# RWKV chunk chain with both heads in one matmul, and the first two input tiles in token halves

## The chip, the cores and the metric

One core of a Trainium2 chip runs one decoder block in fp32. The metric is device time in microseconds of one execution, lower is better. The kernel before takes 2918.94 us (median of 3 runs, 2916.89 to 2919.65).

## The reference, cut to what matters

The block normalises `x` (512 tokens, width 2048), projects it with `w_in`, runs RWKV-7 time mixing and sliding-window attention on parts of the projection, merges them with gates, and ends with a gated convolutional feed-forward. Of this the change touches the projection's beginning and the RWKV recurrence:

```python
h = rms_norm(x, norm1_g[l])
z = h @ w_in[l]
...
def step(state, inp):
    r_t, k_t, v_t, w_t, ka_t, kb_t = inp
    sa = jnp.einsum('bhvk,bhk->bhv', state, ka_t)
    state = (state * w_t[:, :, None, :] + sa[..., None] * kb_t[:, :, None, :]
             + v_t[..., None] * k_t[:, :, None, :])
    y = jnp.einsum('bhvk,bhk->bhv', state, r_t)
    return state, y
```

There are 16 heads of 64 channels. The kernel computes the recurrence in 8 chunks of 64 tokens (`NCH`, `C`), two heads (a pair, 128 partitions) at a time.

## The kernel before, in words

**Projection.** `w_in` is read in column tiles of 128 (`z_tiles`): first the attention keys and values (`c_ka`, `c_va`, two of each), then the queries, the low-rank inputs, and for each pair of heads k, r, v; the 32 gate tiles come last and serve as filler. Every product in fp32 is made of three fp32r matmuls, high times high, low times high, high times low (L259 to L261), 128 by 512 each, 16 input slices `k` to a tile, so 48 matmuls. `load_w` (L237) fetches four slices of weights through a ring of 4 raw buffers and splits them: ACT makes the high part (L244), DVE the low part (L245). After every third call it also issues one step of the running sums that later stages need (`sums_along`, L228 and L229).

**Start.** `x` comes in four row blocks of 128 tokens. Each half of the tokens (two blocks) is squared on ACT (L294), scaled on DVE (L297), turned over by 32 PE transposes (L304) into PSUM tiles `ps_x` of a ring of 6, and split by ACT (`xhi`, L306) and DVE (`xlo`, L307). The first tile's matmuls run over all 512 tokens, so they stand behind both halves.

**RWKV pair.** `early` (L556) makes a pair's inputs, `late` (L616) its chunks. `late` first builds block matrices and inverts a triangular system with fp16 matmuls (L690, L691); then comes the chain over the 8 chunks. For each chunk: `psG` from the state `SV` and `AB`, one matmul for each head into its own 64 partitions (L744); a copy to `G` on DVE (L746); `psU` with the inverse, one matmul for both heads (L748); copies to `UV`, the first head's on ACT (L749), the second's on DVE (L750); `psS`, again a matmul for each head (L755); and the new state on DVE (L757). The chunk's outputs are two more matmuls for each head (L765 with `MM`, L767 with `BAR`), all into one PSUM tile from the ring `bulk` of 3; after the last chunk it is split into `yhl` (L769) for `final`. The unused blocks of `SV` and `UV` hold what the state and the values need beside the own block, so that the contraction over 128 rows gives two terms at once.

**Order.** The framework's scheduler interleaves the engines' streams at build time: the chain's matmuls stand between those of gate and projection tiles. Each engine then runs its own stream strictly in order and waits at semaphores; what stands behind a waiting instruction waits too. Instructions given to `pin` keep their program order.

Of the kernel before, what the change touches and what calls it, by code (L numbers as in the profile page):

```python
# [20 lines left out]
NT = S // P  # L21
HD = 64
C = 64
NCH = S // C
BLK = 128
WIN = 128
RMS_EPS = 1e-6
# [108 lines left out]
def block_kernel(ctx: ExitStack, tc: tile.TileContext, d: Dims, a: dict, out: bass.AP):  # L136
    nc = tc.nc
    act, dve, pool, pe, sync = nc.scalar, nc.vector, nc.gpsimd, nc.tensor, nc.sync
    NK, NP, NQ, NKV, NF = d.NK, d.NP, d.NQ, d.NKV, d.NF
# [16 lines left out]
    ident = const.tile([P, P], F32, name="ident")  # L156
# [5 lines left out]
    cst = cstp.tile([P, NCONST - P], F32, name="cst")  # L162
# [6 lines left out]
    p0 = xin.enter_context(tc.tile_pool(name="x0", bufs=1))  # L169
    xt = [p0.tile([P, d.D], F32, name=f"xi{t}") for t in range(NT)]  # L170
# [35 lines left out]
    def split(hi, lo, src, pin=free):  # L206
        pin(act.activation(hi, src, AF.Copy))
        pin(dve.tensor_tensor(lo, src, hi.bitcast(F32) if hi.dtype == F32R else hi, op=ALU.subtract))
# [28 lines left out]
    def load_w(src):  # L237
# [4 lines left out]
        hi = wp["hl"].tile([P, 512], F32R, name="whi", tag="whi")[:, :n].rearrange("p (k c) -> p k c", c=ncol)  # L242
        lo = wp["hl"].tile([P, 512], F32R, name="wlo", tag="wlo")[:, :n].rearrange("p (k c) -> p k c", c=ncol)
        act.activation(hi, raw, AF.Copy)  # L244
        dve.tensor_tensor(lo, raw, hi.bitcast(F32), op=ALU.subtract)  # L245
        wp["n"] += 1
        if wp["n"] % wp["step"] == 0:
            sums_along()()
        return hi, lo

    def project(acc, src, xhi, xlo, pre=()):
        nk = src.shape[1]
        for k0 in range(0, nk, 4):
            n = min(4, nk - k0)
            whi, wlo = pre[k0 // 4] if k0 // 4 < len(pre) else load_w(src[:, k0 : k0 + n])
            for j in range(n):
                k = k0 + j
                first, last = k == 0, k == nk - 1
                pe.matmul(acc, whi[:, j], xhi[:, k], start=first, stop=False)  # L259
                pe.matmul(acc, whi[:, j], xlo[:, k], start=False, stop=False)  # L260
                pe.matmul(acc, wlo[:, j], xhi[:, k], start=False, stop=last)  # L261


    act.dma_start(par, a["par"])
    sync.dma_start(sinkb, a["attn_sinks"].rearrange("(o h) -> o h", o=1).to_broadcast([P, d.HQ]))
    sync.dma_start(cst, a["cst"][:, P:])
# [17 lines left out]
    if True:  # L284
        xhi = by_k(big(big1, "xhi", "h1"))
        xlo = by_k(big(big1, "xlo", "l1"))
        zt = {c: a["w_z"][i].rearrange("p (k c) -> p k c", c=P) for i, c in enumerate(d.z_tiles())}
        with tc.tile_pool(name="x0_ps", bufs=6, space=PSUM) as ps0:
            ssum = p0.tile([P, NT], F32, name="ssum")
            HT = NT // 2  # L290
            for h in range(2):
                for t in range(h * HT, (h + 1) * HT):
                    sq = p0.tile([P, d.D], F32, name="sqx", tag="sqx", bufs=1)
                    act.activation(sq, xt[t], AF.Square, accum_out=ssum[:, t : t + 1])  # L294
                r = rsqrt_small(p0, ssum[:, h * HT : (h + 1) * HT], 1.0 / d.D, RMS_EPS)
                for t in range(HT):
                    dve.tensor_scalar(xt[h * HT + t], xt[h * HT + t], r[:, t : t + 1], None, op0=ALU.mult)  # L297
            first = {d.c_ka: [load_w(zt[d.c_ka][:, k0 : k0 + 4]) for k0 in range(0, min(NK, 12), 4)]}
            for h in range(2):
                hs = slice(h * HT * P, (h + 1) * HT * P)  # L300
                for k in range(NK):
                    ps = ps0.tile([P, HT * P], F32, name="ps_x", tag="x")
                    for t in range(HT):
                        pe.transpose(ps[:, t * P : (t + 1) * P], xt[h * HT + t][:, k * P : (k + 1) * P], ident)  # L304
                    g = col("n1g", k)
                    act.activation(xhi[:, k, hs], ps, AF.Identity, scale=g)  # L306
                    dve.scalar_tensor_tensor(xlo[:, k, hs], ps, g, xhi[:, k, hs].bitcast(F32), op0=ALU.mult, op1=ALU.subtract)  # L307
        xin.close()
        act.activation(bor, K["bo"], AF.Copy)
        act.activation(cenr, K["cen"], AF.Copy)  # L310

        accp = pa.enter_context(tc.tile_pool(name="accA", bufs=3, space=PSUM, side="right", reuse_waits="tile"))

        def ztile(c0):
            acc = accp.tile([P, S], F32, name="acc", tag="acc")
            project(acc, zt[c0], xhi, xlo, first.pop(c0, ()))
            return acc

        gp = pa.enter_context(tc.tile_pool(name="gate", bufs=1, side="right"))
# [154 lines left out]
        with ExitStack() as pr:  # L474
# [21 lines left out]
            def bulk():  # L496
                return blk.tile([P, S], F32, name="bulk", tag="bulk")
# [42 lines left out]
            def r3(ap, c=C):  # L540
                return ap.rearrange("p (n c) -> p n c", c=c)
# [74 lines left out]
            def late(p, st):  # L616
# [121 lines left out]
                            split(BT[:, 0, ns], BT[:, 1, ns], ps)  # L738


                for n in range(NCH):
                    ps = chn.tile([P, C], F32, name="psG", tag="chn")
                    for h, (lo, hi) in enumerate(HV):
                        pe.matmul(ps[lo:hi], AB[:, n, h], SV[:, n, h], start=True, stop=True)  # L744
                    G = wk.tile([P, C], F32, name="G", tag="G", bufs=2)
                    dve.tensor_copy(G, ps)  # L746
                    ps = chn.tile([P, C], F32, name="psU", tag="chn")
                    pe.matmul(ps, BX[:, n], G, start=True, stop=True)  # L748
                    act.activation(UV[0:C, n, 0], ps[0:C], AF.Copy)  # L749
                    dve.tensor_copy(UV[C:P, n, 1], ps[C:P])  # L750
                    if n == NCH - 1:
                        break
                    ps = chn.tile([P, C], F32, name="psS", tag="chn")
                    for h, (lo, hi) in enumerate(HV):
                        pe.matmul(ps[lo:hi], KK[:, n, h], UV[:, n, h], start=True, stop=True)  # L755
                    for h, (lo, hi) in enumerate(HV):
                        dve.scalar_tensor_tensor(SV[lo:hi, n + 1, h], SV[lo:hi, n, h], ee[lo:hi, n : n + 1], ps[lo:hi],  # L757
                                                 op0=ALU.mult, op1=ALU.add)
# [12 lines left out]

            def final(p, st):
# [621 lines left out]
```

## Time and profile before

| | |
|---|---|
| median of the runs | 2918.94 us |
| profiled execution | 2915.49 us, its span 2913.7 us |
| PE matmul busy | 2868.1 us (98%) |
| DVE, ACT, POOL busy | 1970.2, 1333.6, 219.3 us |
| mean TensorE clock granted | 0.997 |

Rows of the profile give a start (us from the span's beginning), a duration, the engine (PE matmul, PEld weight load, DVE, ACT, SPq and POOLq the queues that issue DMAs), the line, the operation, the tiles as out<-in, the shape and a count. Matmuls are pipelined: a row's duration holds fill and drain, and the next one starts long before it ends. So the cost of a matmul is read from the distance of two starts, not from its duration. An fp32 matmul leaves two records, an fp32r matmul or a transpose one.

### The profile page before, as it was taken

How to read it: one execution, taken by the hardware profiler on the slowest of the kernel's cores; microseconds unless marked ns; L12 is line 12 of the kernel's file. 1: busy time of each engine (PE TensorE's matmuls, PEld its weight loads, DVE VectorE, ACT ScalarE, POOL GpSimd, SP SyncE). 2: the span in 40 equal slices, each digit the busy share in tenths (PEclk: the TensorE clock that was granted, in tenths of full speed). 3: DMA queues.
4: the chain of work that ended last, by engine and by line, in shares of the span. 5: the costliest groups of instructions: out<-in, count | busy, mean ns of one | idle time of the engine just before them, and what ended most of it. 6: DMA issues, size and time to landing. Idle time of an engine off the chain costs nothing.

```text
span 2913.7 us, 46929 instructions
## 1 busy us (share of the span) xinstructions
PE 2868.1 (98%) x18014; PEld 2441.3 (84%) x18014; DVE 1970.2 (68%) x3383; ACT 1333.6 (46%) x2251; POOL 219.3 (8%) x286
## 2 busy tenths in 40 slices
PE   7999999999999999999999899999999999999999
PEld 5777777777777777788888899999999999888887
DVE  4577666667767766354567777787777777665565
ACT  4345435435435434322356455545555455544444
POOL 0001000000000000111000010111111100000000
PEclk9999999999999999999999999999999999999999
DMA  7856756656656655878877788988889888877775
GB/s 210 217 146 166 184 142 168 156 145 163 159 149 149 167 148 139 266 222 239 293 251 226 208 227 231 242 233 231 221 235 238 237 227 234 312 242 240 259 255 188
DMA packets 225137, 609.29 MB, mean 209 GB/s; under 512 B 24768, under 2 KB 44944, under 8 KB 223888
## 3 DMA queue, kind: packets, MB, share of 16 engines
q1 hardware_dynamic: 157504, 434.84, 45.9%
q0 software_dynamic: 36064, 132.14, 23.9%
q10 hardware_dynamic: 31344, 39.31, 4.0%
q8 instruction: 141, 2.31, 0.3%
q14 instruction: 84, 0.69, 0.1%
HBM read 556.54 MB, written 174.43 MB: 251 GB/s over the span
## 4 chain that ended last, share of the span: by engine, by line
PE 94%; DVE 2%; ACT 1%; DMA 1%; issue 0%; SPq 0%; DVEq 0%; ACTq 0%
PE X L1095 17%; PE acc L259 11%; PE X L962 11%; PE acc L261 11%; PE acc L260 11%; PE Y L1095 9%; PE Y L962 8%; PE Z L1095 4%; PE bulk L737 1%; PE bulk L690 1%; PE psG L744 1%; PE bulk L646 1%; PE psS L755 1%; PE mi L464 1%; PE scp L431 1%; PE bulk L554 1%
## 5 line engine op out<-in xcount | busy, mean ns | idle before, releaser
L259 PE MATMUL acc<-xhi,whi 128*128 128x512 f32 x1152 | 473.1, 411 | 5.0 <-ACT whi L244 3.1
L261 PE MATMUL acc<-xhi,wlo 128*128 128x512 f32 x1152 | 469.2, 408 | 0.0
L260 PE MATMUL acc<-xlo,whi 128*128 128x512 f32 x1152 | 467.1, 405 | 0.0
L244 ACT ACTIVATE whi<-raw 128x512 fp32r<-128x512 f32 x352 | 220.3, 630 | 492.8 <-PE acc L260 376.6
L955 DVE TENSOR_TENSOR wlo<-raw,whi 128x1024 fp32r<-128x1024 f32 x210 | 257.0, 1224 | 204.9 <-ACT whi L954 203.4
L245 DVE TENSOR_TENSOR wlo<-raw,whi 128x512 fp32r<-128x512 f32 x352 | 240.2, 689 | 207.3 <-ACT whi L244 195.4
L954 ACT ACTIVATE whi<-raw 128x1024 fp32r<-128x1024 f32 x210 | 222.8, 1061 | 287.9 <-PE X L962 147.1
L1095 PE MATMUL X<-b,whi 128*128 128x256 f32 x1472 | 270.2, 284 | 2.2 <-DVE u L1115 0.9
L1095 PE MATMUL X<-t,whi 128*128 128x256 f32 x1408 | 260.2, 285 | 8.7 <-DVE u L1115 8.3
L1078 DVE TENSOR_TENSOR wlo<-raw,whi 128x1024 fp32r<-128x1024 f32 x176 | 215.0, 1222 | 77.4 <-ACT whi L1077 77.2
L259 PEld LDWEIGHTS acc<-xhi,whi 128*128 128x128 f32 x1152 | 217.5, 189 | 52.8 <-ACT whi L244 4.4
L261 PEld LDWEIGHTS acc<-xhi,wlo 128*128 128x128 f32 x1152 | 217.3, 189 | 48.2 <-issue 2.2
L1095 PE MATMUL Y<-t,whi 128*128 128x256 f32 x1408 | 257.5, 283 | 0.0
L260 PEld LDWEIGHTS acc<-xlo,whi 128*128 128x128 f32 x1152 | 217.7, 189 | 44.9 <-issue 3.3
L1077 ACT ACTIVATE whi<-a 128x1024 fp32r<-128x1024 f32 x132 | 139.4, 1056 | 213.8 <-DVE a L1071 211.2
L1095 PEld LDWEIGHTS X<-b,whi 128*128 128x128 f32 x1472 | 230.3, 193 | 3.0 <-issue 2.3
L1095 PEld LDWEIGHTS X<-t,whi 128*128 128x128 f32 x1408 | 222.0, 194 | 9.3 <-DVE u L1115 5.7
L1095 PEld LDWEIGHTS Y<-t,whi 128*128 128x128 f32 x1408 | 220.1, 192 | 0.0
L1095 PE MATMUL X<-b,wlo 128*128 128x256 f32 x736 | 208.9, 284 | 2.1 <-DVE wlo L1078 2.1
L1078 DVE TENSOR_TENSOR wlo<-a,whi 128x1024 fp32r<-128x1024 f32 x132 | 161.7, 1225 | 67.7 <-ACT whi L1077 67.0
L1095 PE MATMUL X<-t,wlo 128*128 128x256 f32 x704 | 200.5, 285 | 0.0
L1095 PE MATMUL Y<-t,wlo 128*128 128x256 f32 x704 | 199.3, 283 | 0.0
(345 smaller groups left out, 5877.7 us busy)
## 6 DMA issues: line engine op xcount, KB each, us to landing
raw<-in_w_up_dram SPq DMA_DIRECT2D x180, 512.0 KB
raw<-in_w_z_dram SPq DMA_DIRECT2D x288, 256.0 KB
s_dn<-in_w_dn_dram POOLq DMA_DIRECT2D x88, 512.0 KB, 6.7
raw<-in_w_up_dram POOLq DMA_DIRECT2D x88, 512.0 KB, 8.1
raw<-s_dn SPq DMA_DIRECT2D x88, 512.0 KB
raw<-in_w_dn_dram SPq DMA_DIRECT2D x66, 512.0 KB
a<-in_w_up_dram SPq DMA_DIRECT2D x48, 512.0 KB
s_dn<-in_w_dn_dram SPq DMA_DIRECT2D x44, 512.0 KB
```

Source lines behind the costliest of these rows:

```text
L244: act.activation(hi, raw, AF.Copy)
L245: dve.tensor_tensor(lo, raw, hi.bitcast(F32), op=ALU.subtract)
L259: pe.matmul(acc, whi[:, j], xhi[:, k], start=first, stop=False)
L260: pe.matmul(acc, whi[:, j], xlo[:, k], start=False, stop=False)
L261: pe.matmul(acc, wlo[:, j], xhi[:, k], start=False, stop=last)
L431: pe.matmul(scp[e][:, j, k0:], qn[j][hs, ts], kd[g][hs, n * P - BLK + k0 : (n + 1) * P], start=True, stop=True)
L954: act.activation(whi, wr, AF.Copy)
L955: dve.tensor_tensor(wlo, wr, whi.bitcast(F32), op=ALU.subtract)
L962: pe.matmul(dst, l[:, q, ts], r[:, es], start=fst and j == 0, stop=lst and j == 2, skip_group_check=True)
L1077: pin(act.activation(hi, t, AF.Copy))
L1078: pin(dve.tensor_tensor(lo, t, hi.bitcast(F32), op=ALU.subtract))
L1095: pin(pe.matmul(ps, l[:, k], r[:, k], start=start and k + i == 0, stop=last and i == 2, skip_group_check=True))
```

## The change

**In the chain**, the two matmuls of `psG`, of `psS`, and of each output become one of 128 by 128 over both heads (`heads2`). The result then holds four blocks of 64 by 64; the two that belong to one head each are read, the others are not. `G` is copied in two halves, the first on ACT, the second on DVE. The outputs go to two PSUM tiles of four chunks each, and each of these is split in two halves of 64 partitions.

**At the start**, the first two tiles (`c_ka`, `c_va`) have PSUM accumulators of their own and are computed in token halves of 256 (`half_mm`), with an order that is pinned: all of half 0 turned over, tile 0 on half 0, then half 1 turned over with tile 1 on half 0 between, then both tiles on half 1. Their weights stay in a pool of 8 buffers each. One block of half 1 is scaled on ACT. The constants (`cst`, `sinkb`) are fetched after the first weights. The count that sets `sums_along` begins at 8, with an extra step at 31 and at 34; the ring `ps_x` has 5 buffers.

```diff
-    wp = {"n": 0, "step": 3}
+    wp = {"n": 2 * NK // 4, "step": 3}
...
-        if wp["n"] % wp["step"] == 0:
+        if wp["n"] % wp["step"] == 0 or wp["n"] in (31, 34):
             sums_along()()
...
+            def half_mm(i, h, k):
                 hs = slice(h * HT * P, (h + 1) * HT * P)
+                whi, wlo = (w[:, k % 4] for w in ws[i][k // 4])
+                for j, (l, r) in enumerate(((whi, xhi), (whi, xlo), (wlo, xhi))):
+                    pin(pe.matmul(heads[i][:, hs], l, r[:, k, hs], start=h == 0 and k + j == 0,
+                                  stop=k == NK - 1 and j == 2, skip_group_check=True))
...
+            for k in range(NK):
+                columns(0, k)
+                if k == NK // 2 - 1:
+                    r = scales(1)
+                if k >= NK // 2 and k % 2:
+                    weights(0, 2 * (k - NK // 2 - 1))
+            for t in range(HT):
+                scaled(1, t, r, act if t else dve)
+            sync.dma_start(cst, a["cst"][:, P:])
+            sync.dma_start(sinkb, a["attn_sinks"].rearrange("(o h) -> o h", o=1).to_broadcast([P, d.HQ]))
+            for k in range(NK):
+                half_mm(0, 0, k)
+            for k in range(NK):
+                if k % 4 == 0:
+                    weights(1, k)
+                columns(1, k)
+                half_mm(1, 0, k)
+            for i in range(2):
                 for k in range(NK):
+                    half_mm(i, 1, k)
...
                 for n in range(NCH):
-                    ps = chn.tile([P, C], F32, name="psG", tag="chn")
-                    for h, (lo, hi) in enumerate(HV):
-                        pe.matmul(ps[lo:hi], AB[:, n, h], SV[:, n, h], start=True, stop=True)
+                    ps = chn.tile([P, 2, C], F32, name="psG", tag="chn")
+                    pe.matmul(heads2(ps), heads2(AB[:, n]), heads2(SV[:, n]), start=True, stop=True)
                     G = wk.tile([P, C], F32, name="G", tag="G", bufs=2)
-                    dve.tensor_copy(G, ps)
+                    act.copy(G[0:C], ps[0:C, 0])
+                    dve.tensor_copy(G[C:P], ps[C:P, 1])
...
-                    for h, (lo, hi) in enumerate(HV):
-                        pe.matmul(ps[lo:hi], KK[:, n, h], UV[:, n, h], start=True, stop=True)
+                    pe.matmul(heads2(ps), heads2(KK[:, n]), heads2(UV[:, n]), start=True, stop=True)
...
-                ps = bulk()
-                for n in range(NCH):
+                yhl = wk.tile([P, 2, S], F32R, name="yhl", tag="rhl")
+                for g in range(2):
+                    ps = bulk().rearrange("p (n h c) -> p n h c", h=2, c=C)
+                    for j in range(HN):
+                        n = g * HN + j
+                        pe.matmul(heads2(ps[:, j]), heads2(UV[:, n]), heads2(MM[:, n]), start=True, stop=n == 0)
+                        if n:
+                            pe.matmul(ps[:, j], heads2(SV[:, n]), BAR[:, n, :, 1], start=False, stop=True)
                     for h, (lo, hi) in enumerate(HV):
-                        dst = r3(ps)[lo:hi, n]
-                        pe.matmul(dst, UV[:, n, h], MM[:, n, h], start=True, stop=n == 0)
-                        if n:
-                            pe.matmul(dst, SV[:, n, h], BAR[:, n, h, 1], start=False, stop=True)
-                yhl = wk.tile([P, 2, S], F32R, name="yhl", tag="rhl")
-                split(yhl[:, 0], yhl[:, 1], ps)
+                        own = [r3(yhl[lo:hi, e])[:, g * HN : (g + 1) * HN] for e in range(2)]
+                        split(own[0], own[1], ps[lo:hi, :, h])
```

The order of PE's instructions in the first pair's chain, before: the state and outputs of one chunk and the `psG` of the next. `acc` is a projection or gate tile, the filler, and the sizes are those of the output:

```order
L755 MATMUL psS<-UV,KK 64x64
L765 MATMUL bulk<-MM,UV 64x64
L767 MATMUL bulk<-BAR,SV 64x64
L259 MATMUL acc<-xhi,whi 128x512
L755 MATMUL psS<-UV,KK 64x64
L765 MATMUL bulk<-MM,UV 64x64
L767 MATMUL bulk<-BAR,SV 64x64
L260 MATMUL acc<-xlo,whi 128x512
L261 MATMUL acc<-xhi,wlo 128x512
L744 MATMUL psG<-SV,AB 64x64
L259 MATMUL acc<-xhi,whi 128x512
L744 MATMUL psG<-SV,AB 64x64
```

The same engine at the same place after the change, one whole chunk:

```order
L792 MATMUL psG<-SV,AB 128x128
L263 MATMUL acc<-xhi,wlo 128x512
L261 MATMUL acc<-xhi,whi 128x512
L262 MATMUL acc<-xlo,whi 128x512
L797 MATMUL psU<-G,BX 128x64
L263 MATMUL acc<-xhi,wlo 128x512
L261 MATMUL acc<-xhi,whi 128x512
L262 MATMUL acc<-xlo,whi 128x512
L803 MATMUL psS<-UV,KK 128x128
L814 MATMUL bulk<-MM,UV 128x128
L816 MATMUL bulk<-BAR,SV 128x128
```

The matmuls with 64 output partitions are gone. Before, the two heads' matmuls could stand apart with filler between them, here two stretches for the state and outputs and two for `psG`; now a chunk has one stretch for `psG`, one for `psU` and one for state and outputs, with three fillers between the first two and between the second two.

ACT's stream in the same chain before the change; beside the copies to `UV` it holds the weights' high parts and `early`'s activations:

```order
L749 ACTIVATE UV<-psU 64x64 x2
L580 ACTIVATE lw<-bulk 128x512
L244 ACTIVATE whi<-raw 128x512
L749 ACTIVATE UV<-psU 64x64
L586 ACTIVATE Et<-bulk 128x8x64
L588 ACTIVATE Ei<-bulk 128x512
```

And after it:

```order
L794 COPY G<-psG 64x64
L798 ACTIVATE UV<-psU 64x64
L794 COPY G<-psG 64x64
L244 ACTIVATE whi<-raw 128x512
L798 ACTIVATE UV<-psU 64x64
L207 ACTIVATE yhl<-bulk 64x256
```

Each chunk has one more ACT instruction (`G`, whose other half, L795 on DVE, waits for the ACT half in the built program), and the first output split stands within the chain.

At the start, PE's stream before, where the first tile's matmuls begin (`xi` is a block of `x`; 162 and 163 are those of half 1):

```order
L304 MATMUL ps_x<-ident,xi_162 128x128
L304 MATMUL ps_x<-ident,xi_163 128x128
L259 MATMUL acc<-xhi,whi 128x512
L260 MATMUL acc<-xlo,whi 128x512
L261 MATMUL acc<-xhi,wlo 128x512
```

And after the change (160 and 161 are the blocks of half 0):

```order
L314 MATMUL ps_x<-ident,xi_160 128x128
L314 MATMUL ps_x<-ident,xi_161 128x128
L326 MATMUL acc<-xhi,whi 128x256
L326 MATMUL acc<-xlo,whi 128x256
L326 MATMUL acc<-xhi,wlo 128x256
```

48 half-width matmuls now stand behind the 32 transposes of half 0; before, the first matmul stood behind all 64 transposes.

More of the change, by code (lines that the diff above doesn't have):

```diff
@@ L241, in load_w, with project @@
         wp["last"] = sync.dma_start(raw, src)
[L242 to L245, printed above, removed]
+        hi, lo = ((pl or wp["hl"]).tile([P, 512], F32R, name=nm, tag=nm, bufs=bufs)[:, :n].rearrange("p (k c) -> p k c", c=ncol)
+                  for nm in ("whi", "wlo"))
+        pin(act.activation(hi, raw, AF.Copy))
+        pin(dve.tensor_tensor(lo, raw, hi.bitcast(F32), op=ALU.subtract))
+        if pl:
+            return hi, lo
         wp["n"] += 1
-        if wp["n"] % wp["step"] == 0:
+        if wp["n"] % wp["step"] == 0 or wp["n"] in (31, 34):
             sums_along()()
         return hi, lo
-    def project(acc, src, xhi, xlo, pre=()):
+    def project(acc, src, xhi, xlo):
         nk = src.shape[1]
@@ L254, in project @@
             n = min(4, nk - k0)
-            whi, wlo = pre[k0 // 4] if k0 // 4 < len(pre) else load_w(src[:, k0 : k0 + n])
+            whi, wlo = load_w(src[:, k0 : k0 + n])
             for j in range(n):
@@ L287, in block_kernel @@
         zt = {c: a["w_z"][i].rearrange("p (k c) -> p k c", c=P) for i, c in enumerate(d.z_tiles())}
-        with tc.tile_pool(name="x0_ps", bufs=6, space=PSUM) as ps0:
+        accp = pa.enter_context(tc.tile_pool(name="accA", bufs=3, space=PSUM, side="right", reuse_waits="tile"))
+        heads = [accp.tile([P, S], F32, name="acc", tag="acc") for _ in range(2)]
+        first = dict(zip((d.c_ka, d.c_va), heads))
+        with tc.tile_pool(name="x0_ps", bufs=5, space=PSUM) as ps0:
             ssum = p0.tile([P, NT], F32, name="ssum")
@@ L298, in block_kernel @@
-            first = {d.c_ka: [load_w(zt[d.c_ka][:, k0 : k0 + 4]) for k0 in range(0, min(NK, 12), 4)]}
-            for h in range(2):
-                hs = slice(h * HT * P, (h + 1) * HT * P)
-                for k in range(NK):
[L302 to L307, printed above, removed]
+            for t in range(NT):
+                sq = p0.tile([P, d.D], F32, name="sqx", tag="sqx", bufs=1)
+                act.activation(sq, xt[t], AF.Square, accum_out=ssum[:, t : t + 1])
@@ new lines, in scales, with scaled, columns @@
+            def scales(h):
+                return rsqrt_small(p0, ssum[:, h * HT : (h + 1) * HT], 1.0 / d.D, RMS_EPS)
+            def scaled(h, t, r, eng):
+                x = xt[h * HT + t]
+                if eng is dve:
+                    pin(dve.tensor_scalar(x, x, r[:, t : t + 1], None, op0=ALU.mult))
+                else:
+                    pin(act.activation(x, x, AF.Copy, scale=r[:, t : t + 1]))
+            def columns(h, k):
+                hs = slice(h * HT * P, (h + 1) * HT * P)
+                ps = ps0.tile([P, HT * P], F32, name="ps_x", tag="x")
+                for t in range(HT):
+                    pin(pe.transpose(ps[:, t * P : (t + 1) * P], xt[h * HT + t][:, k * P : (k + 1) * P], ident))
+                g = col("n1g", k)
+                pin(act.activation(xhi[:, k, hs], ps, AF.Identity, scale=g))
+                pin(dve.scalar_tensor_tensor(xlo[:, k, hs], ps, g, xhi[:, k, hs].bitcast(F32), op0=ALU.mult, op1=ALU.subtract))
@@ new lines, in block_kernel @@
+            r = scales(0)
+            for t in range(HT):
+                scaled(0, t, r, dve)
+            ws = [[], []]
+            for k in range(NK):
[4 more added lines that the diff above has]
+                    weights(0, 2 * (k - NK // 2 - 1))
+            for t in range(HT):
+                scaled(1, t, r, act if t else dve)
+            sync.dma_start(cst, a["cst"][:, P:])
+            sync.dma_start(sinkb, a["attn_sinks"].rearrange("(o h) -> o h", o=1).to_broadcast([P, d.HQ]))
@@ L308, in block_kernel @@
+            for k in range(NK):
[6 more added lines that the diff above has]
+            for i in range(2):
+                for k in range(NK):
+                    half_mm(i, 1, k)
         xin.close()
[L309 to L312 removed]
+        pin(act.activation(bor, K["bo"], AF.Copy))
@@ L314, in ztile @@
+        pin(act.activation(cenr, K["cen"], AF.Copy))
         def ztile(c0):
+            if c0 in first:
+                return first.pop(c0)
             acc = accp.tile([P, S], F32, name="acc", tag="acc")
-            project(acc, zt[c0], xhi, xlo, first.pop(c0, ()))
+            project(acc, zt[c0], xhi, xlo)
             return acc
```

22 lines of the change are left out of this document (9 added, 13 removed).

## The prediction

> **What bounds the kernel now.** I read the page's busy shares and its chain that ended last, then the stages by windows, then PE's timeline within one RWKV chunk.
>
> ```profile
> PE 2868.1 (98%) x18014; PEld 2441.3 (84%) x18014; DVE 1970.2 (68%) x3383; ACT 1333.6 (46%) x2251; POOL 219.3 (8%) x286
> ...
> PE 94%; DVE 2%; ACT 1%; DMA 1%; issue 0%; SPq 0%; DVEq 0%; ACTq 0%
> ```
>
> ```profile
> 14.80:34.60 19.80, 14.15 (x64) 11.03 (x64) 19.27 (x51) 16.02 (x39) 1.82 (x2) 1.00 0.76 220
> 34.60:37.80 3.20, 3.13 (x7) 2.48 (x8) 0.01 (x1) 0.00 (x0) 0.00 (x0) 0.50 0.08 14
> 345.00:1175.00 830.00, 828.00 (x5480) 624.22 (x5479) 554.82 (x1345) 359.77 (x805) 53.28 (x67) 1.00 0.61 154
> ```
>
> PE ends the chain for 94% of the span, and it is busy for 828.0 of the 830 us in which the eight RWKV chains run (columns: PE, PEld, DVE, ACT, POOL, granted clock, DMA share, GB/s). So a microsecond taken from PE's stream in that stage is a microsecond of the kernel, unless something else becomes late. The stage from 14.8 to 34.6 us is different: there DVE is busy for 19.27 of 19.80 us, and PE stands between its transposes.
>
> "Busy" hides what PE does in the chain. The price of a piece of the stream is the distance of two starts. First the plain prices, from a place without the chain:
>
> ```profile
> 317.80 0.39 PE L261 MATMUL acc<-xhi,wlo 128*128 128x512 f32 x1
> ...
> 318.49 0.39 PE L261 MATMUL acc<-xhi,wlo 128*128 128x512 f32 x1
> ...
> 318.92 1.05 PE L578 MATMUL bulk<-wl,thw 128*128 128x128 f32 x8
> 319.73 0.48 PE L259 MATMUL acc<-xhi,whi 128*128 128x512 f32 x1
> 320.05 0.39 PE L260 MATMUL acc<-xlo,whi 128*128 128x512 f32 x1
> ```
>
> Three `acc` steps take 0.69 us, 0.23 each. Eight records of full-width fp32 with 128 columns take 0.81, and the `acc` behind them is followed 0.09 late (0.32 for 0.23): 0.90 in all, 0.1125 a record, with nothing left for the edges. Now the chain, with filler between:
>
> ```profile
> 395.01 0.40 PE L261 MATMUL acc<-xhi,wlo 128*128 128x512 f32 x1
> ...
> 395.94 0.50 PE L259 MATMUL acc<-xhi,whi 128*128 128x512 f32 x1
> 396.29 0.40 PE L260 MATMUL acc<-xlo,whi 128*128 128x512 f32 x1
> 396.61 0.34 PE L744 MATMUL psG<-SV,AB 128*64 128x64 f32 x4
> 396.88 0.50 PE L261 MATMUL acc<-xhi,wlo 128*128 128x512 f32 x1
> 397.22 0.40 PE L259 MATMUL acc<-xhi,whi 128*128 128x512 f32 x1
> 397.45 0.33 PE L748 MATMUL psU<-G,BX 128*128 128x64 f32 x2
> ...
> 397.91 0.40 PE L261 MATMUL acc<-xhi,wlo 128*128 128x512 f32 x1
> ...
> 398.73 0.49 PE L259 MATMUL acc<-xhi,whi 128*128 128x512 f32 x1
> ```
>
> ```profile
> 399.64 0.50 PE L260 MATMUL acc<-xlo,whi 128*128 128x512 f32 x1
> 399.98 0.40 PE L261 MATMUL acc<-xhi,wlo 128*128 128x512 f32 x1
> 400.30 0.33 PE L744 MATMUL psG<-SV,AB 128*64 128x64 f32 x2
> 400.56 0.51 PE L259 MATMUL acc<-xhi,whi 128*128 128x512 f32 x1
> 401.00 0.33 PE L744 MATMUL psG<-SV,AB 128*64 128x64 f32 x2
> 401.26 0.27 PE L337 MATMUL bulk<-ident,rq 128*8 128x128 f32 x1
> ```
>
> Take the `acc` steps out and the prices remain. State and outputs of both heads in one stretch: 395.01 to 396.29 is 1.28, less 0.46, 0.82 us. `psG` of both heads in one stretch: 396.29 to 397.22, 0.47. `psU`, which is 128 wide already: 397.22 to 397.91, 0.23. State and outputs, one head at a time: 397.91 to 399.98 is 2.07, less three steps, 1.38. `psG` apart: 399.98 to 401.26 is 1.28, less 0.46, and 0.10 for the late step that follows where an `acc` stands behind: 0.92.
>
> So a stretch of matmuls with 64 output partitions has an edge that a stretch of 128 hasn't: 0.09 before it, 0.05 within, 0.09 behind it, and 0.10 at the next `acc`, about 0.34 us. The edge behind falls on `acc` matmuls that wait for no data. The row at 396.61 also shows the gain of this form: four records, two for each head, pass in 0.27 us, hardly more than two alone at 400.30 (0.26).
>
> **The chain, part by part.** Counted in the trace, the 64 chunks (eight pairs of eight) have `psG` in one stretch 28 times and apart 36 times; state and outputs of the 48 inner chunks in one stretch 21 times, apart 27 times. The first chunks have no `SV` output, the last no state: I estimate 8 x 0.7 and 8 x 1.2, between the rows above. Before: 28 x 0.47 + 36 x 0.92 + 21 x 0.82 + 27 x 1.38 + 15 = 13 + 33 + 17 + 37 + 15 = 115 us.
>
> After, the chain has 64 `psG`, 56 `psS`, 64 and 56 outputs, each one full-width instruction of two records: 480 x 0.1125 = 54 us, and 2 for edges, 56. The bounds of the edge are 0, as at 318.92, and 0.1 us for each of the 128 stretches, 13 us. Saved: 59, between 46 and 61. The same account by the median distance of every pair of neighbours, over all starts of the window row above, gives 119 before and 53 after, 66 saved. I take 62.
>
> Then the chain's own wait. The copy of `G` is now ACT's half and, after it, DVE's.
>
> ```profile
> 393.27 0.33 PE L744 MATMUL psG<-SV,AB 128*64 128x64 f32 x2
> 393.63 0.22 DVE L746 COPY G<-psG 128x64 f32<-128x64 f32 x1 [0.64 <-PE psG L744]
> 394.55 0.33 PE L748 MATMUL psU<-G,BX 128*128 128x64 f32 x2
> 394.92 0.22 ACT L749 ACTIVATE UV<-psU 64x64 f32<-64x64 f32 x1 [3.31 <-PE psU L748]
> 395.17 0.23 DVE L750 COPY UV<-psU 64x64 f32<-64x64 f32 x1 [0.58 <-ACT UV L749]
> ```
>
> ACT follows `psU` by 0.37, DVE follows ACT by 0.25 and takes 0.23. With `psG`'s second record later by 0.06, and twice the columns, `psU` can start some 1.00 us after `psG`; what stands between (0.22 of `psG` and three fillers, 0.69) lasts 0.91. That is a wait of 0.09 x 64, at most 6 us; I take 4. From `psU` to `psS` the same chain needs 0.90, and 0.92 stands between. From `psS` to the next `psG` two DVE updates must pass, about 1.1 us, and six records and two fillers last 1.13. All three are covered with nothing to spare, so an ACT or DVE instruction that happens to stand ahead shows on PE. If cover fails everywhere, see the first rival.
>
> The output split becomes four pieces on ACT and four on DVE for a pair instead of one each, perhaps 0.9 us more on each engine; ACT is busy for 360 and DVE for 555 of the 830 us, so they take it up, except where the two early ones stand ahead of a chain copy: at most 0.4 x 2 x 8 = 6 us, in the range.
>
> **The start.**
>
> ```profile
> 17.03 0.48 DVE L307 SCALAR_TENSOR_TENSOR xlo<-ps_x,par,xhi 128x256 fp32r<-128x256 f32 x1 [0.31 <-ACT xhi L306]
> ...
> 19.01 0.69 DVE L245 TENSOR_TENSOR wlo<-raw,whi 128x512 fp32r<-128x512 f32 x1
> ...
> 22.35 2.47 DVE L297 TENSOR_SCALAR xi<-xi,rq 128x2048 f32<-128x2048 f32 x2
> 24.74 9.87 DVE L307 SCALAR_TENSOR_TENSOR xlo<-ps_x,par,xhi 128x256 fp32r<-128x256 f32 x25
> ```
>
> ```profile
> 34.67 0.79 PE L259 MATMUL acc<-xhi,whi 128*128 128x512 f32 x1 [1.91 <-DVE xlo L307]
> ```
>
> ```profile
> 1693.82 5.76 PE X L1095 x48
> ```
>
> Before, the first tile starts at 34.67, runs 3.2 us at a granted clock of 0.50 (a loss of 1.6) and two tiles are 96 x 0.23: they would end at 58.4. After, PE may begin when the last transposes of half 0 have a buffer, which by the ring of 5 is when DVE has made 11 columns: from 17.03, 11 x 0.395 (9.87 over 25), one weight split of 0.69 and some 2 us of small operations, 24.1, plus 0.4 for the transposes: 24.5. From there 192 half-width matmuls at 0.12 (5.76 over 48) are 23.0, the 32 transposes that now stand in the stream 3.6, the same half clock 1.6, edges 1: 53.7. Gain 4.7; I take 4.5. DVE must still make 21 columns (8.3), about 11 weight splits (7.6) and one scaling (1.2), so it ends near 41, ahead of PE's need. Bounds: nothing, if DVE or the weights hold PE up after all, and 6.
>
> The moved DMAs: `cst` and `sinkb` wait on SP's queue behind four weight loads, and the first that needs them stands at the end of this phase, 20 us later. The first running sum moves from the start to the third tile, with its partner on POOL's queue, and is caught up by the steps at 31 and 34; its result is read after 1240 us. I price both at nothing.
>
> **Sum.** The profiled execution took 2915.5: 2915.5 - 62 + 4 - 4.5 = 2853. The runs' median lies 3.4 above that execution, so 2856.
>
> **Rivals.** *ACT is late.* `G` now waits in ACT's queue.
>
> ```profile
> L244 ACT ACTIVATE whi<-raw 128x512 fp32r<-128x512 f32 x352 | 220.3, 630 | 492.8 <-PE acc L260 376.6
> ```
>
> A weight split of 0.63 that stands ahead delays the chunk by up to that. With 0.5 us on each of 64 chunks, 32 us are given back: 2888. For it: the thin cover. Against: ACT is busy for 43% of the stage, and `UV` went through it already.
>
> *The chain is data-bound, and the edge is a wait.* The tile view of `psG` names a releaser:
>
> ```profile
>   DVE SV L757: 12.7, 36
> ```
>
> If the edges before were waits for `SV` and `UV`, they stay (115 less 47 of streaming, 68 us), the streaming becomes 54 because the second head no longer passes beside the first, and the second half of `G` adds 0.25 x 64 = 16: 138 for 115, 23 slower, 4.5 less by the start: 2937. It decides from about 1 us more wait for each chunk (62 over 64). Against: the distance is the same 0.32 at 399.98 and at 396.29, and the edge behind, on fillers, has no data to wait for.
>
> The Trainium skill speaks for this side: its page "TensorEngine Tiling (Array Packing)", section Theoretical Speedup, gives up to twice the speed where an operand has 64 columns or fewer, because two tiles work at once. The trace agrees in the row at 396.61. By that rule alone the merged matmuls would cost some 27 us more; the same page's Key Properties say that a change of the tiling mode drains the array, which fits the edges, and the trace prices that higher.
>
> *The edge belongs to the change from fp32r to fp32*, not to the width, so the merge doesn't remove it. Then 128 stretches keep 0.34: 44 + 54 = 98 for 115, 2901 with waits and start. Against: `psU` and L578 are fp32 at full width and have no such edge.
>
> **How the numbers follow.** Forecast 0.76 (2838 to 2874, own bounds of edges, waits and start); ACT late 0.12; edge by type 0.04; data-bound 0.05; a gain beyond 80 us 0.03. The range reaches from 2838 to 2890. What a measurement can tell from no change is about 0.2%, 6 us: faster 0.94, same 0.01, slower 0.05.
>
> **What would show it.** The stage of the chains (830 us) should be about 58 shorter; around each `psG`, `psS` and output the next `acc` should start 0.1125 after the last record, without the 0.32 ahead. Distances over 1.1 us from `psG` to `psU` would show the wait, with ACT named. The first half-width matmul should start near 24.5, the third tile be alone on PE from near 54. Wrong would make it: edges of 0.3 that stay on full-width stretches, or DVE's idle before `G` growing.

## The result, and the profile after

The changed kernel takes 2940.7 us (median; 2932.45 to 2945.7) against 2917.9 us of the kernel before (2916.8 to 2919.65) on the same chip: ratio 1.0075, 95% interval 1.0051 to 1.0099. It is some 23 us slower by the medians, where 63 us less was forecast. The profiled execution took 2932.45 us, its span 2930.7 us.

The same two rows of the page as before, now of the changed kernel:

```profile
PE 2847.7 (97%) x17630; PEld 2445.0 (83%) x17630; DVE 1980.0 (68%) x3406; ACT 1351.7 (46%) x2340; POOL 218.9 (7%) x286
...
PE 87%; DVE 6%; DMA 4%; issue 1%; ACT 1%; SPq 0%; ACTq 0%; DVEq 0%
```

PE is busy for 20.4 us less (2868.1 before), yet its share of the chain that ended last falls from 94 to 87%: DVE goes from 2 to 6, DMA from 1 to 4. PE was spared work, and then waits for others. The window of the chains says where (columns as before, the granted clock stands ahead of the DMA share):

```profile
341.50:1203.20 861.70, 818.85 (x5033) 631.89 (x5031) 565.30 (x1371) 377.73 (x897) 53.90 (x68) 0.98 0.61 150
```

The stage of the chains lasts 861.7 us instead of 830. PE stands idle for 43 us of it (2 before), and its clock there is 0.98 (1.00 before). The view of PE's waits names them, first for the kernel before, then for the changed one (what waited, releaser: us in total, times, longest):

```profile
PE bulk L337 <- DVE rq L198: 0.6, 2, 0.4
PE bulk L646 <- DVE MM L650: 0.3, 1, 0.3
```

```profile
PE bulk L691 <- DVE MM L695: 18.4, 7, 5.6
PE bulk L656 <- DVE lw L654: 18.3, 7, 3.0
PE bulk L382 <- DVE rq L198: 3.9, 8, 0.5
```

None of these lies in the chain. L656 is the `bo` matmul of early(p+1), which needs `rk` (tile `lw`). L691 are the first matmuls of late(p+1), whose `bulk` tiles are freed by DVE's AB and MM (L694, L695). L382 is the small transpose of `head_rows` itself. The chain that ended last, followed through the first of these waits, tells what stands behind them:

```profile
413.55 0.38 SPq L390
413.98 3.24 DMA rsb<-rsd
417.25 0.69 DVE kk L617
417.97 0.42 DVE yhl L208
...
419.81 0.69 DVE kz L652
...
421.11 0.67 DVE lw L654
421.92 1.19 PE bulk L656 x2
...
436.13 4.12 DMA rsd<-rsT
...
440.79 3.18 DMA rsb<-rsd
...
445.36 0.46 DVE yc L836
445.82 0.33 DVE AB L694
446.15 0.60 DVE yc L837
446.75 0.34 DVE MM L695
447.23 1.97 PE bulk L691 x8
```

Read from the bottom of each half: PE waits for DVE, DVE works off a queue, and the queue stood at a product (`kk*rb` at L617, `yc*rb` at L835) whose rows were on their way through DRAM. `head_rows` turns a pair's scales over on PE, copies them out as `rsT`, stores them (4.12 us in the second half above) and loads them back, each row spread over 64 partitions (3.2 us). DVE's own timeline has the two products, with its idle time ahead of them:

```profile
417.25 0.69 DVE L617 TENSOR_TENSOR kk<-kk,rsb 128x512 f32<-128x512 f32 x1 [2.46 <-DMA rsb<-rsd]
444.07 0.69 DVE L835 TENSOR_TENSOR yc<-yc,rsb 128x512 f32<-128x512 f32 x1 [2.62 <-DMA rsb<-rsd]
```

Each pair makes two such trips. What changed most is what PE has to do meanwhile. Between the transpose of the first trip and the `bo` matmul the trace has 29 `acc` and 45 other matmuls before (36 of these the chain's), and 28 and 17 after (8 of the chain); between the transpose of the second and the first AB/MM matmul 53 `acc` before, and 24 after. PE needed 17.5 us for the first of these stretches and 14.2 for the second; now it gets through what stands there in some 12 and 7.4.

The products themselves start about as long after the `rsT` copy as they did: `kk*rb` 8.5 to 9.2 us before and 8.6 to 9.6 after, `yc*rb` 9.0 to 11.3 before and 7.7 to 12.8 after. But for `kk*rb` the reason is another one. Before, the loads of the first trip went out 3.1 us after the copy, and DVE, busy with other work, hardly waited for the rows. After, they go out 5.0 to 6.0 us behind it, since the store takes longer to land (SP waits 51.9 us for the stores of the stage, 12.9 before), and DVE stands idle. The view of `rsb`, first before, then after (who waited for it: us, times):

```profile
  DVE kk L572: 1.4, 3
```

```profile
  DVE kk L617: 16.8, 7
```

So the wait before `bo` has two parts, less cover and a slower store; gates4 below shows that 12 us of cover are enough for a trip whose product starts after 6.8.

Within the chain the change did what it was made for. PE's timeline of one chunk, after:

```profile
391.08 0.39 PE L262 MATMUL acc<-xlo,whi 128*128 128x512 f32 x1
391.35 0.46 PE L792 MATMUL psG<-SV,AB 128*128 128x128 f32 x2
391.56 0.48 PE L263 MATMUL acc<-xhi,wlo 128*128 128x512 f32 x1
391.88 0.39 PE L261 MATMUL acc<-xhi,whi 128*128 128x512 f32 x1
392.11 0.40 PE L262 MATMUL acc<-xlo,whi 128*128 128x512 f32 x1
392.36 0.44 PE L797 MATMUL psU<-G,BX 128*128 128x64 f32 x2
392.61 0.48 PE L263 MATMUL acc<-xhi,wlo 128*128 128x512 f32 x1
392.92 0.39 PE L261 MATMUL acc<-xhi,whi 128*128 128x512 f32 x1
```

`psG` costs 391.08 to 391.88 less two steps, 0.34 us (0.47 or 0.92 before); `psU` 392.11 to 392.92 less two steps, 0.35 (0.23 before).

An account of the whole stage, worked out from the trace, holds these apart. Taken are all distances of neighbouring matmul starts from 40 records ahead of the first `psG` to 40 behind the last `cenr`, less 0.2305 us for each that begins at an `acc`; the fillers' own time, of which after has 36 matmuls (8.3 us) more in its stage, is so taken out. The two experiments in the last columns come below.

| us | before | after | rows_after | products_late |
|---|---|---|---|---|
| next to a chain matmul or an output | 118.5 | 80.1 | 77.1 | 80.0 |
| from `acc` to `acc`, beyond 0.2305 | 35.0 | 39.2 | 30.0 | 27.5 |
| all others | 162.8 | 220.8 | 182.9 | 174.6 |
| sum | 316.3 | 340.1 | 290.0 | 282.1 |

The chain gives 38 us, and the rest of the stage takes 62: some 40 more of the waits above (40.6 against 0.9), and most of the remainder, 19 us, by the half clock that follows such a wait (37.5 us of the stage ran at a granted clock of 0.50, none of it before). One such wait and the stretch behind it:

```profile
418.80:421.90 3.10, 0.45 (x2) 0.03 (x2) 3.04 (x6) 0.63 (x1) 0.00 (x0) 1.00 0.32 84
421.90:425.30 3.40, 3.38 (x8) 2.39 (x9) 3.04 (x5) 0.45 (x1) 0.00 (x0) 0.63 0.74 214
```

Over the program the granted clock is 0.990 for 0.997, which over 2930 us is 20 us.

### The profile page after: what moved, and what is told of

It reads as the page before. It is cut to its first block, busy times and chain, and to the rows that moved or that the text cites. A ratio compares the mean times of both kernels' runs of the same rounds, so it can differ in the third digit from the quotient of the medians.

```text
span 2930.7 us, 46335 instructions
## 1 busy us (share of the span) xinstructions
PE 2847.7 (97%) x17630; PEld 2445.0 (83%) x17630; DVE 1980.0 (68%) x3406; ACT 1351.7 (46%) x2340; POOL 218.9 (7%) x286
## 4 chain that ended last, share of the span: by engine, by line
PE 87%; DVE 6%; DMA 4%; issue 1%; ACT 1%; SPq 0%; ACTq 0%; DVEq 0%
PE X L1145 17%; PE X L1012 11%; PE acc L262 9%; PE acc L261 9%; PE acc L263 9%; PE Y L1012 8%; PE Y L1145 8%; PE Z L1145 4%; DMA rsb<-rsd 2%; DMA rsd<-rsT 2%; DVE wlo L245 1%; PE bulk L735 1%; PE bulk L782 1%; PE mi L509 1%; PE bulk L691 1%
## 5 line engine op out<-in xcount | busy, mean ns | idle before, releaser
L261 PE MATMUL acc<-xhi,whi 128*128 128x512 f32 x1120 | 457.9, 409 | 0.0
L262 PE MATMUL acc<-xlo,whi 128*128 128x512 f32 x1120 | 456.9, 408 | 0.0
L263 PE MATMUL acc<-xhi,wlo 128*128 128x512 f32 x1120 | 455.1, 407 | 0.0
```

## The experiments

The theory: the chain's price on PE did fall, but the loop over the pairs then stands at two round trips through DRAM that PE's longer stream, and an order with more fillers behind the transposes, had covered. The rivals: the start lost the time; G, which ACT now copies by half, comes late; the merged matmul is dearer than forecast. Lines in the profiles are each kernel's own; "before" is the kernel before on the same chip.

**The two parts apart.** chain_alone has L784 to L820 of the changed kernel in the kernel before, start_alone has the new start and the old chain:

```diff
-                    for h, (lo, hi) in enumerate(HV):
-                        pe.matmul(ps[lo:hi], AB[:, n, h], SV[:, n, h], start=True, stop=True)
+                    pe.matmul(heads2(ps), heads2(AB[:, n]), heads2(SV[:, n]), start=True, stop=True)
...
-                    for h, (lo, hi) in enumerate(HV):
-                        pe.matmul(ps[lo:hi], KK[:, n, h], UV[:, n, h], start=True, stop=True)
+                    pe.matmul(heads2(ps), heads2(KK[:, n]), heads2(UV[:, n]), start=True, stop=True)
```

> The kernel before, with the merged chain matmuls and outputs alone; the start of the input projection is as before. TensorE's order from the first chain on is the one of the changed kernel, instruction for instruction. Theory (the chain part makes the loop over the pairs wait for the two round trips through DRAM, some 42 us of waits and 19 us of half clock, and the start gains its 4.5 us as forecast): 2945 us, about 4 above the changed kernel, and waits of TensorE at L656's and L691's counterparts of 18 us each. Rival (the start lost the time): 2855 to 2865 us.

2949.65 us, ratio 1.011 (1.0088 to 1.0132). Its waits of PE in the chain stage:

```profile
PE bulk L646 <- DVE MM L650: 26.3, 7, 5.5
PE bulk L611 <- DVE lw L609: 19.9, 7, 3.3
```

> The kernel before with the token halves at the start alone; the chain and the outputs are as before. Theory (the loss lies in the chain part): 2913 us, 4 to 5 below the kernel before, no waits over 1 us in the chain stage. Rival (the start lost the time, by a transfer or a sum moved into the chain stage): 2935 us or more.

2912.72 us, ratio 0.9985 (0.9974 to 0.9996); no wait is over 1.2 us in the stage. The loss belongs to the chain part, and the start is no rival.

**No round trip.** rows_after spreads the scales over rows by four matmuls against the identity, without a store and a load; rows_before does the same in the kernel before.

```diff
+        def rows_on_pe(pl, ps, rs, tag):
+            rx = pl.tile([P, NT, 2, HD], F32, name="rsx", tag=tag)
+            dve.tensor_copy(rx, rs.rearrange("p (h t) -> p t h", h=2).unsqueeze(3).to_broadcast([P, NT, 2, HD]))
+            for t in range(NT):
+                pe.matmul(ps[:, t * P : (t + 1) * P], rx[:, t].rearrange("p h c -> p (h c)"), ident, start=True, stop=True)
+            return ps
...
-                rb = head_rows(wk, bulk(), rs, "lg")
+                rb = rows_on_pe(wk, bulk(), rs, "lg")
...
-                rb = head_rows(wk, bulk(), rs, "gn")
+                rb = rows_on_pe(wk, bulk(), rs, "gn")
```

> The changed kernel, with the head scales of the RWKV part spread over rows by four matmuls against the identity into PSUM and one DVE copy, in place of a transpose, a store to DRAM and two loads. TensorE's order is within a few instructions of the changed kernel's. Costs 8 x 2 x (four 128-wide records for one) = about 6 us of TensorE. Theory (the round trips are what TensorE waits for): the waits before L656 and L691 (18 us each) and the half clock behind them (19 us) go, 2940 - 37 - 19 + 6 = 2890 us, between 2875 and 2905. Rival (the chain waits for ACT, which now copies G, or merged matmuls are dearer than forecast): within 10 us of 2940.

> The kernel before with the same replacement of the round trips by matmuls. Theory (before the change they were covered, since TensorE waited for less than 1 us there): 2920 to 2930 us, the added records' 6 us and no gain. Rival (the round trips cost time before as well): below 2905.

rows_after: 2884.2 us, ratio 0.9891 (0.9871 to 0.9911). rows_before: 2921.25 us, 1.0015 (1.0005 to 1.0024). The longest group in the view of PE's waits of rows_after is now a weight split, and the window of its chains has the clock back:

```profile
PE bulk L664 <- ACT whi L244: 1.8, 6, 0.3
```

```profile
338.80:1148.30 809.50, 805.25 (x5124) 629.35 (x5123) 568.31 (x1370) 377.84 (x896) 54.06 (x68) 1.00 0.62 154
```

So some 54 to 56 us (by the ratios, by the medians) hang on the two trips in the changed kernel, and none in the kernel before. PE's order is almost the same as in the changed kernel (again 24 or 25 `acc` between the second scale and AB/MM), so it costs time only with a trip to wait for.

**Only the first trip.** rows_kk replaces the one for `kk`, not the one for `yc`.

> The changed kernel with only the first of a pair's two round trips (the scale of kk) replaced by matmuls into PSUM. Theory (two separate waits of 18 us each, each with some 9 us of half clock behind it): the waits before L656 go, those before L691 stay near 18 us: 2940 - 19 - 9 + 3 = 2915 us, between 2905 and 2925. Rival (one wait feeds the other, so that one cure is enough): 2890 us or less.

2911.68 us, ratio 0.9985 (0.9972 to 0.9998). The wait before `bo` is gone, the other stands:

```profile
PE bulk L699 <- DVE MM L703: 17.0, 7, 4.6
```

These are two waits, and each costs about half.

**Other amounts of filler.** gates4 sets GATES_PER_PAIR, the gate tiles that a pair has as filler, from 3 to 4. chain_noout and out_only have one part of the merge each: the first keeps the outputs of before, the second `psG` and `psS` of before. G_dve copies both halves of G by DVE:

```diff
-GATES_PER_PAIR = 3
+GATES_PER_PAIR = 4
```

```diff
-                    act.copy(G[0:C], ps[0:C, 0])
+                    dve.tensor_copy(G[0:C], ps[0:C, 0])
```

> The changed kernel with four gate tiles emitted per pair instead of three, so that the eight that followed the last pair are used as filler within the pairs. In the planned order 66 acc matmuls stand between the transpose of the second head_rows of a pair and the first AB/MM matmul of the next (24 in the changed kernel, 53 before); between the transpose of the first head_rows and the bo matmul stand 28, as in the changed kernel. Theory (each wait is the round trip less the filler behind it, about 8.2 us less 0.23 a matmul): the waits before L691 go (18 us and some 9 of half clock), those before L656 stay near 18 us, and the last pair, which now has no filler, loses some 8: 2920 us, between 2910 and 2930. Rival (the chain itself is late through G on ACT): no change, 2935 to 2945.

2926.64 us, ratio 1.0031 (1.0019 to 1.0044). In the stage no wait before L691 is left; before L656 stand 8.1 us, less than the 18 expected, since some of its trips are shorter: `kk*rb` starts 6.8 to 9.0 us after the copy, and the two pairs at 6.8 have no wait, with the changed kernel's 28 `acc` and 12 us of cover:

```profile
PE bulk L656 <- DVE lw L654: 8.1, 5, 2.3
```

The time is inside the range, but not all by the way foreseen: the last pair, without filler, costs more than the 8 us estimated. In the view of its last 100 us PE waits for the first tile of the stage behind it:

```profile
PE acc L261 <- ACT rhi L207: 13.3, 1, 13.3
```

> The changed kernel with psG and psS merged, but the outputs as before (one tile, two matmuls of 64 partitions a head, one split). The planned order falls back nearly to that of before: 48 acc matmuls between the second transpose and AB/MM, 23 acc and 26 chain records between the first transpose and bo. Theory: the waits before AB/MM go, those before bo are 1 to 2 us a pair, psG saves some 20 us of TensorE: 2910 us, between 2895 and 2920. Rival (G in ACT's queue, or the merged matmul with its late weight load, is the loss): 2930 us or more.

2898.84 us, ratio 0.9932 (0.9913 to 0.995), faster than the 2910 expected: no wait before `bo`, and one of 0.8 us before AB/MM. The merged `psG` is the same instruction as in the changed kernel, and with `SV` in time it costs what was forecast (387.68 to 388.37 less two steps, 0.23), at all 35 places where fillers stand on both sides. `psU` costs 0.23 where `G` is early, as here with four fillers ahead of it (388.83 to 389.52), at 20 of 50 such places, and 0.36 at the others:

```profile
387.68 0.40 PE L263 MATMUL acc<-xhi,wlo 128*128 128x512 f32 x1
387.91 0.39 PE L792 MATMUL psG<-SV,AB 128*128 128x128 f32 x2
388.05 0.48 PE L261 MATMUL acc<-xhi,whi 128*128 128x512 f32 x1
388.37 0.39 PE L262 MATMUL acc<-xlo,whi 128*128 128x512 f32 x1
...
388.83 0.40 PE L261 MATMUL acc<-xhi,whi 128*128 128x512 f32 x1
389.07 0.33 PE L797 MATMUL psU<-G,BX 128*128 128x64 f32 x2
389.21 0.48 PE L262 MATMUL acc<-xlo,whi 128*128 128x512 f32 x1
389.52 0.40 PE L263 MATMUL acc<-xhi,wlo 128*128 128x512 f32 x1
```

> The changed kernel with the outputs merged, in two tiles with four splits, and psG and psS as before, one matmul for each head. The planned order resembles that of the changed kernel, with 36 acc matmuls (24) between the second transpose and AB/MM and 31 (28) before bo. Theory: no waits before AB/MM, some 2 us a pair before bo with their half clock, about 19 us, against some 10 us saved on the outputs and 4 at the start: 2923 us, between 2910 and 2935. Rival (the order of the chain's own copies is the loss): 2905 us or less, since these are as before.

2932.33 us, ratio 1.0045 (1.0032 to 1.0058). PE waits 11.3 us before `bo` and, where none was expected, 4.0 before AB/MM. So the order with fewer fillers comes mainly with the merged outputs (36 `acc` ahead of AB/MM here, 48 in chain_noout, 24 with both). By the account above, the chain's row is 106.4 us in chain_noout and 112.5 in out_only, against 118.5 and 80.1: each part alone saves 12 or 6, both 38. State and outputs share a stretch, so its edge would go only when the whole stretch is 128 wide; this fits the numbers, and no run tests it by itself.

> The changed kernel with both halves of G copied by DVE, none by ACT. The planned order has 0 to 17 acc matmuls between the second transpose and AB/MM, in place of 24, and in four pairs 35 instead of 28 before bo. Theory: the waits before L691 grow to some 35 us (8.2 less 0.23 for each matmul), those before L656 shrink to some 12: 2955 us, between 2945 and 2970. Rival (a G that waits behind weight splits in ACT's queue is the loss): 2920 us or less.

2915.54 us, ratio 0.9986 (0.9971 to 1.0001): a miss by 40 us, and the time that the rival gave. Its waits show that my count of fillers was not the whole of it:

```profile
PE bulk L707 <- DVE BX L700: 13.6, 6, 3.1
PE bulk L656 <- DVE lw L654: 6.4, 3, 2.2
PE bulk L691 <- DVE MM L695: 3.9, 1, 3.9
```

In this program's order, from the second turn of the loop on, two or all four of a pair's AB/MM products stand ahead of `yc*rb` on DVE, not all behind it. So AB/MM hardly wait for the trip, however few fillers there are, and the wait moves on to the transposes of BX (L707), behind `yc*rb`. The rival's reason isn't in it: the chain's row is 84.6 us, 4.5 more than with ACT's help, so the half on ACT was no loss.

**The trips kept, their users moved.** This is the direct test. products_late leaves both trips as they are, and places only the products later: `kk*rb` behind the `rsT` copy of the second head_rows, `yc*rb` behind the AB/MM products. `rk` gets a buffer of its own, since `lw` was shared with `ta`, which `kb` must read first.

```diff
-                dve.tensor_tensor(kk, kk, rb, op=ALU.mult)
...
-                kb = kz
-                dve.tensor_tensor(kb, kk, ta, op=ALU.mult)
-                rk = wtile("lw")
+                rk = wtile("rk")
...
+                def scaled_keys():
+                    pin(dve.tensor_tensor(kk, kk, rb, op=ALU.mult))
+                    dve.tensor_tensor(kz, kk, ta, op=ALU.mult)
...
+                    pin(dve.tensor_tensor(yc, yc, rb, op=ALU.mult))
...
-                final(p, lt)
+                rest = final(p, lt)
+                if p + 1 < NP:
+                    keys()
```

(`keys` is scaled_keys of early; `rest`, the part of final from `yc*rb` on, is called in late behind the AB/MM loop.)

> The changed kernel with its round trips through DRAM left as they are, and only the products that need them traced and kept later on DVE: kk*rb behind the rsT copy of the second head_rows, yc*rb behind the AB/MM products of the next pair; rk has a buffer of its own, since it shared one with ta, which kb reads. In the planned order kk*rb then stands some 44 acc matmuls and 14 others behind the first transpose, yc*rb some 45 acc and AB/MM behind the second. No TensorE work is added or removed. Theory (TensorE waits because DVE stands at a product whose rows are still in flight, with what it needs queued behind): the waits before L656 and L691 and the half clock behind them go, 2940 - 37 - 19 = 2884 us, between 2870 and 2895. Rival (the trips cost time themselves, through SP's queue or the DMA engines, or the chain is the loss): 2925 us or more.

> The kernel before with the same later products. Theory (before the change nothing waited there): 2918 us, within 6. Rival (the later place is better in itself, by shorter waits of any kind): 2905 us or less.

products_late: 2875.23 us, ratio 0.9862 (0.9846 to 0.9879), the fastest of all. products_late_before: 2914.03 us, 0.9998 (0.9989 to 1.0008). In products_late the stage, its clock and PE's longest group of waits are:

```profile
345.60:1142.20 796.60, 791.89 (x5002) 614.37 (x5000) 563.61 (x1369) 376.92 (x894) 53.17 (x67) 1.00 0.65 161
```

```profile
PE bulk L709 <- ACT AI L207: 1.7, 5, 0.4
```

The same trips, as many matmuls, and 65 us less than the changed kernel (62 by the ratios), while the same move gives the kernel before nothing. The rebuilt program does place PE's fillers differently. Between the first transpose and `bo` stand 14 `acc`, not 28, so `bo` has less cover than in the changed kernel (8.6 us, not 12) and still no wait. Ahead of AB/MM stand 45, not 24, so there the move isn't alone; but the first such stretch has 23, without a wait, and rows_after has 24 or 25. The loads are issued as late as in the changed kernel, 3.8 to 5.9 us after the first copy. That settles the cause: DVE stood at a product in flight, and what PE needed was queued behind it.

## Why the prediction was wrong

**What bounds the kernel.** The step that failed is the sentence "a microsecond taken from PE's stream in that stage is a microsecond of the kernel, unless something else becomes late". The condition was then tested for the chunk alone: "All three are covered" speaks of `psG`, `psU` and `psS`. The distances within a chunk were not the only ones that PE's stream covered. The two trips of a pair had 17.5 and 14.2 us of PE's work over them; after the change 12 and 7.4 us stand over products that start 8.6 to 9.6 and 7.7 to 12.8 us after the copy, with DVE's queue still behind them (4.5 us from the start of `kk*rb` at 417.25 to `rk`'s end at 421.78). The order of the changed program, of which one chunk was looked at, holds the answer further on: 24 `acc` of 0.23 are 5.5 us, less than a trip. The rivals named ACT and SV, both inside the chunk; none named a DMA.

**The chain's price.** The mechanism, an edge around each stretch of 64 partitions, was right; the term was too large. Forecast was 62 less 4. Measured are 38 next to chain matmuls, and some 8 more in the late `acc` steps behind the edges (35.0 to 27.5 in products_late, where no half clock hides it): 46, the low end of the bounds. What fell short is above all the term "I take 4" for the chain's own wait. `psG` to `psU` was forecast at 1.00 us and is 1.01 (391.35 to 392.36), but a matmul whose operand comes at the last moment costs more than the time it is late: 0.34 for 0.23 at `psG`, 0.35 for 0.23 at `psU`. Together that would be 0.23 us on each of 64 chunks, 15 us; an estimate, as 35 `psG` and 41 `psU` were measured so, between fillers.

**The start.** Right: the first half-width matmul is at 24.21 (24.5 forecast), and the chain stage begins 4.2 us sooner, at 341.5 (4.5 forecast). The two tiles end at 56.3 (53.7 forecast), and before at 60.1 (58.4 forecast). start_alone measures 3.1 us, 2915.81 less 2912.72.

```profile
24.21 0.56 PE L326 MATMUL acc<-xhi,whi 128*128 128x256 f32 x1
```

Until then DVE is busy for 8.55 of 9.40 us, as the forecast had it, but ACT, which it did not count, for 8.74:

```profile
14.80:24.20 9.40, 6.46 (x32) 5.47 (x33) 8.55 (x28) 8.74 (x20) 0.00 (x0) 0.96 0.41 155
```

**The rivals.** "ACT is late": no, by G_dve's chain row. "The edge belongs to the change from fp32r to fp32": no, by chain_noout, whose `psG` costs 0.23. "The chain is data-bound" named 2937, close to the outcome, but by a chain that grows by 23, and its row fell by 38: that the time is near is chance. The loss came by a way that had no chance in the forecast.

**The sum.** 2915.5 − 38 (chain) + 62 (waits, half clock) − 4 (start) = 2935 for 2932.45 measured; the last 3 us lie behind the stage and were not traced further. With the trips covered, 2884.2 and 2875.2 stand beside the 2856 of the forecast; the 19 us between the last two are the 12 that the chain gave too little (46 for 58) and 7 not accounted for.

What stays open: why the built order puts fewer fillers behind the transposes when the outputs are merged. out_only shows that it comes with them, not by what rule. Nor is it known why the store of the first trip takes longer to land in the changed kernel.

## What to carry to other kernels

Before you take time out of the engine that bounds a loop, list every transfer whose result comes back within it (here two a pair, with the product 8 to 13 us behind the copy), and count in the new order what that engine does between each issue and its first user; what you take out was their cover. Count on the queue of the engine that uses the result as well: one product in flight holds up all that is queued behind it, and to place it later cost nothing here (products_late_before, ratio 0.9998). Look at the whole period of the loop, not only at the piece that is changed.

## What the runs showed of the hardware

Half clock came after a short idle: PE was idle for 2.65 of the 3.10 us from 418.80 to 421.90, and the `acc` steps behind ran at 0.43 instead of 0.23:

```profile
423.96 0.43 PE acc L261
424.38 0.43 PE acc L262
```

Of the eleven waits of 2 us or more in the changed kernel's stage the nine of 2.5 to 5.6 us were followed by it, those of 2.0 and 2.4 us were not.

The Trainium skill, page "TensorE: Matmul & The Clock Gate", section HAM oscillation — how this bites in real kernels, names idle gaps above about 3.4 us as the ones to avoid. The trace agrees in kind, but here shorter ones were enough, so each wait of some 3 us cost more than itself.

A full-width fp32 matmul of two records cost 0.23 us where its operand was early and 0.34 where it came just in time, at no idle time that the profile shows. It is seen in the distance of the starts alone. In the changed kernel `psU` cost 0.36 at the 41 places where `G` was written 0.1 us or less ahead of it, and 0.23 at the nine where its operands were earlier.
